# Transposing the MLP activations of a decoder trunk by transfers through a DRAM scratch

## The chip, the cores and the metric

One core of one Trainium2 chip runs the kernel. The metric is the device time of one execution in microseconds. Before the change three runs took 2196.67, 2196.99 and 2197.36 us; their median is 2196.99 us. A run-to-run difference of about 0.2% (4.4 us) is what a measurement of this kernel can tell from no change.

## What is computed

The reference is a decoder trunk of two layers over 256 tokens of width 2048, in float32. Each layer does a self-attention, a cross-attention over 256 memory tokens, and a squared-ReLU MLP with 8192 hidden columns; each is pre-normed and added to the residual stream. The change touches the MLP alone:

```python
def sq_relu_mlp(h, wup, wdown):
    return jnp.square(jax.nn.relu(h @ wup)) @ wdown
...
x = x + sq_relu_mlp(rms_norm(x, mlp_norm[i]), mlp_wup[i], mlp_wdown[i])
```

The product with `wup` leaves tokens on the partitions and hidden columns along the row. The product with `wdown` sums over hidden columns, so TensorE wants these on the partitions: each activated tile of 128 tokens x 512 hidden columns has to be turned between the two.

## The kernel before

**Arithmetic.** Every float32 matrix is held as two parts, a high one (`hi`, the value rounded to the type that TensorE reads in one pass) and a low one (`lo`, value minus `hi`), and a product is three matmuls: hi x hi, hi x lo, lo x hi. ScalarE (ACT) makes the high part of a weight by a cast (`whi`, line 219), VectorE (DVE) the low part by a subtraction (`wlo`, line 220). A weight tile `raw` of 128 x 2048 elements (1 MB) gives two such *pieces* of 128 x 1024 each. There are seven `raw` buffers, and four buffers for each of `whi` and `wlo`, so ACT and DVE run at most four pieces ahead of TensorE. Transfers of weights are issued by SyncE (SP) in program order (`load`, line 187); some 1 MB transfers that add onto a loaded tile are issued by GpSimd (POOL, lines 840 and 964).

**The MLP.** The hidden columns are worked in eight blocks `b` of 1024, each of two chunks `c` of 512, for two token tiles `t` of 128. Block 0 is done plainly. Blocks 1 to 7 use seven products in place of eight (class `Seven`, products `p1` to `p7` in the order p1 p1 p5 p5 p6 p3 p6 p3 p2 p7 p2 p7 p4 p4, two steps each; a step is two pieces of six matmuls). Sums of the products leave four activated tiles in each block, in the order p6, p1, p5, p4. The down product of earlier blocks (`mm` in a profile's rows, twelve matmuls for each piece) is laid between the steps of `Seven` (`pr`).

**The activated tile.** `out` (in `mlp`, lines 1403 to 1428) starts one task for each activated tile. The task does ReLU and a square on ACT (lines 1416 and 1417; the name of a tile tells its product, p6 for example, which the profile shows as `p`), waits some planned time, takes a free PSUM bank, turns the tile by four transposes of 128 x 128 on TensorE (`transpose4`, lines 372 to 376; `flip`, line 172), and reads the bank into the two parts of a tile `unit` (`split`, lines 360 to 365: a cast on ACT, line 364, and a subtraction on DVE, line 365). Down products that come later read this `unit`.

**What sets the order.** TensorE's order is written out by the program: side tasks such as `out` say with `yield` how long they mean to wait on a planned clock (`T_SQ`, `T_TURN` and so on), and are stepped in between matmuls when that time has come. The instructions of the other engines are put in order by a scheduler with its own idea of their durations; each engine then takes its queue strictly in order. SP's weight loads keep the program's order among themselves. Small float32 tiles (activated tiles among them) come from seven rotating buffers, tag `ev`.

Of the kernel before, what the change touches and what calls it, by code (L numbers as in the profile page):

```python
# [10 lines left out]
F32 = mybir.dt.float32  # L11
F32R = mybir.dt.float32r
I32 = mybir.dt.int32
AF = mybir.ActivationFunctionType
ALU = mybir.AluOpType
AX = mybir.AxisListType

P = 128
# [3 lines left out]
CH = 512  # L22
# [4 lines left out]
LAST = MLP_BLOCKS - 1  # L27
SEVEN = (1, 2, 3, 4, 5, 6, 7)
SPREAD = {("p1", 1), ("p5", 1), ("p6", 0), ("p6", 1), ("p2", 0), ("p2", 1), ("p7", 1)}
EVS = 7  # L30
WEAVE = "A1", "A2", "A5", "A3", "A6 B1", "A7 B2", "A4", "B5", "B3", "B6", "B7", "B4"
CLOSING = "u A1 u A2 B1 u A5 B2 u B5 u A6 u A3 B6 u B3 u A7 A4 u B7 u B4"

T_EV, T_TURN, T_ROT, T_SM, T_SQ, T_ADD, T_NORM, T_SUM = 2.6, 2.6, 12.0, 6.5, 4.4, 2.2, 7.2, 3.0

URGENT = 250
NEG = -1.0e30
# [14 lines left out]
def trunk(ctx, tc, x, xT, xT0, mem, memT, positions, gcols, gfinal, lam_vecs, consts, W, out):  # L52
    nc = tc.nc

    def pool(name, bufs, space=None):
        kw = {"space": space} if space else {}
        return ctx.enter_context(tc.tile_pool(name=name, bufs=bufs, **kw))
# [5 lines left out]
    work = pool("work", 2)  # L63
    small = pool("small", 3)
    banks = pool("banks", 8, bass.MemoryType.PSUM)

    serial = [0]

    def nm(s):
        serial[0] += 1  # L70
        return f"{s}_{serial[0]}"
# [102 lines left out]
    def f32(ap):  # L174
        return ap.bitcast(F32)
# [173 lines left out]
    g = keep.tile([P, NG], F32, name="g")  # L349
    pos = keep.tile([P, NT], I32, name="pos")  # L350
    lamv = work.tile([P, 4, P], F32, tag="ev", name="lamv", bufs=EVS)
# [8 lines left out]
    def split(dst, t, src):  # L360

        n = src.shape[1]
        hi = dst[:, 0, :n, t * P : (t + 1) * P]
        nc.scalar.copy(hi, src)  # L364
        nc.vector.tensor_tensor(dst[:, 1, :n, t * P : (t + 1) * P], src, f32(hi), ALU.subtract)  # L365

    def scaled(src, cols, tmp=None):
        if tmp is None:
            tmp = work.tile([P, 4, P], F32, tag="ev", name=nm("xg"), bufs=EVS)
        nc.vector.tensor_tensor(tmp, src, cols.unsqueeze(2).broadcast_to([P, 4, P]), ALU.mult)  # L370
        return tmp

    def transpose4(src, pt):

# [20 lines left out]
    def given_tile(dst, k, raw, gain):  # L395
        nc.scalar.activation(dst[:, 0, k], raw, AF.Copy, scale=gain)
        given_low(dst, k, raw, gain)
# [5 lines left out]
    def sum_squares(acc, src, scale=1.0):  # L403
        junk = work.tile([P, CH], mybir.dt.bfloat16, tag="junk", name=nm("junk"), bufs=1)
        return nc.scalar.activation(junk[:, : src.shape[1]], src, AF.Square, scale=scale, accum_out=acc)  # L405

# [121 lines left out]
    def evacuate(ps, scale):  # L528
        e = work.tile([P, CH], F32, tag="ev", name=nm("ev"), bufs=EVS)
        nc.scalar.activation(e[:, : ps.shape[1]], ps, AF.Copy, scale=scale)  # L530
        return e
# [868 lines left out]
    def mlp(l, norm, gnext):  # L1400
        a = norm.done()
        rstd = keep2(norm.rstd, 1.0, "r1")
        hid = {}

        chunk = {}
        sums = {}
        copied = {}

        def out(b, c, t, src, r, wait):

            if (b, c) not in hid:
                hid[b, c] = Held(unit())
            dst = hid[b, c]

            def task():
                nc.scalar.activation(r, src, AF.Relu, scale=rstd[t])
                nc.scalar.activation(r, r, AF.Square)
                yield wait
                pt = yield from side_bank()
                pt = transpose4(r, pt)  # L1420
                if b < LAST or (t, c) != (1, 0):
                    split(dst, t, pt)
                if b == LAST:
                    pair.keep(t, c, pt)
                yield T_TURN
                give_back()

            dst.run(task())

        def finish_chunk(of, ps, landed):  # L1430
            for t in range(NT):
                if of.kind == "up":
                    r = work.tile([P, CH], F32, tag="ev", name=nm("ev"), bufs=EVS)
                    out(*of.halves[0], t, ps[t], r, T_SQ)
                else:
                    add_residual(t, of.c, ps[t])
                    if landed:
                        landed(of.c, t, ps[t], True)

        def acts_of(of):  # L1440
            if of.kind == "up":
                return [a.unit_of(u) for u in range(4)]
            return [hid[k] for k in of.halves]

        def run(line, landed=None):
            for item in line:
                of = item.of
                if item.early:
                    item.early(hid)
                if isinstance(of, Seven):  # L1450
                    of.products(
                        a, item.u, copied,
                        lambda t, c, src, r, b=of.b: out(b, c, t, src, r, T_SQ + 7.0),
                    )
                    continue
                if isinstance(of, Pair):
                    of.products([hid[LAST, c] for c in range(2)], item.u, landed)
                    continue
                n = len(of.all)
                if item.u == 0:  # L1460
                    if of.open:
                        sums[of.kind, of.c] = [bank("mm") for _ in range(NT)]
                    chunk["acts"] = acts_of(of)
                act = chunk["acts"][item.u]
                need(act.tasks)
                for h, (hi, lo) in enumerate(take()):
                    for t in range(NT):
                        unit_part(sums[of.kind, of.c][t], act, h, hi, lo, t, of.open and item.u == 0, of.close and item.u == n - 1)
                if item.u == n - 1 and of.close:
                    finish_chunk(of, sums.pop((of.kind, of.c)), landed)  # L1470

        line, end, pair = mlp_lines[l]
        limit = free_banks[0] - 1
        free_banks[0] -= limit
        run(line)

        def last(nxt):
            left = {(c, t): 1 for c in range(4) for t in range(NT)}
            for item in end:
                if isinstance(item.of, Pair):  # L1480
                    for t, j, _ in Pair.ADDS[item.u]:
                        left[item.of.cols[j], t] += 1

            def landed(c, t, ps, alone, side=None):
                if side == 0:
                    assert left[c, t] == 1
                    nxt(c, t, ps, side)
                    return
                left[c, t] -= 1
                if not left[c, t]:  # L1490
                    assert alone
                    nxt(*((c, t, ps) if side is None else (c, t, ps, side)))

            run(end, landed)
            assert not any(left.values())
            free_banks[0] += limit

        if gnext is None:
            return last
        nxt = Stream(gnext)  # L1500
        last(nxt.feed)
        return nxt
# [344 lines left out]
```

## Time and profile before

| | |
|---|---|
| median of three runs | 2196.99 us |
| the profiled execution | 2197.04 us |
| its span, first to last instruction | 2195.3 us |
| granted TensorE clock, mean | 0.999 |
| TensorE matmuls busy | 2184.3 us (100%) |
| VectorE busy | 1742.1 us (79%) |
| ScalarE busy | 1409.1 us (64%) |
| GpSimd busy | 177.1 us (8%) |
| DMA, two main queues | 51.3% and 19.9% of 16 engines' time |

Times in the rows are from the start of the span. In a timeline a row gives start, length, engine, source line, operation, tiles (output <- inputs), how many were merged, and in brackets the idle time before it with what ended it. Matmuls overlap in the pipe, so the distance between two starts tells how long TensorE gives to one, and not the length of a row. `SPq` is SP's queue of issues. A table of windows gives the busy time of each engine in a stretch. In the list of transfers the last number is the median time from issue to landing.

### The profile page before, as it was taken

Reading aid. Unit: us, or ns where it says so; the run is one execution under the profiler, and the core shown is the slowest. Engines: PE = TensorE matmul, PEld = TensorE weight load, DVE = VectorE, ACT = ScalarE, POOL = GpSimd, SP = SyncE. Lnnn points to the kernel's source line nnn. Section 1 sums busy time; section 2 is a strip of 40 time slices with the busy share of each in tenths; the row PEclk is TensorE's granted clock in tenths of the full one; section 3 lists DMA queues with packets and bytes.
Section 4 is the critical chain, followed back from the end, with each engine's and each line's share of the span. In section 5 each row is a group of like instructions: output and inputs, shape, how many; then the busy total and the mean of one; then the engine's idle time right before and its main releaser. Section 6 shows DMA issues by size and latency. Waiting matters only on the chain.

```text
span 2195.3 us, 27641 instructions
## 1 busy us (share of the span) xinstructions
PE 2184.3 (100%) x10451; PEld 1831.1 (83%) x10451; DVE 1742.1 (79%) x1962; ACT 1409.1 (64%) x1872; POOL 177.1 (8%) x270
## 2 busy tenths in 40 slices
PE   9999999999999999999999999999999999999998
PEld 7888888888888888888889988888888888888887
DVE  6665878788888788878886878778887887888887
ACT  7555656666766766666765755556766667666665
POOL 1112210000000000000000320000000000000001
PEclk9999999999999999999999999999999999999999
DMA  9447796447967887797996344635878679779795
GB/s 384 157 158 251 213 292 235 159 153 242 310 210 228 294 236 227 266 278 229 294 252 221 105 165 155 248 127 184 266 262 265 203 284 288 212 242 294 230 311 149
DMA packets 76886, 509.28 MB, mean 232 GB/s; under 512 B 8784, under 2 KB 9168, under 8 KB 17872
## 3 DMA queue, kind: packets, MB, share of 16 engines
q1 hardware_dynamic: 64800, 422.83, 51.3%
q0 software_dynamic: 11520, 83.89, 19.9%
q8 instruction: 82, 1.34, 0.2%
q10 hardware_dynamic: 432, 0.79, 0.1%
q14 instruction: 52, 0.43, 0.1%
HBM read 505.38 MB, written 2.10 MB: 231 GB/s over the span
## 4 chain that ended last, share of the span: by engine, by line
PE 98%; DVE 1%; DMA 0%; issue 0%; ACT 0%; DVEq 0%; POOLq 0%; POOL 0%
PE mm L168 63%; PE pr L168 29%; PE ax L168 3%; PE ax L172 2%; PE mm L172 1%; DVE wlo L220 0%; DMA raw<-in_mlp_wup_dram 0%; DMA raw<-in_da_wqkv_dram 0%; DVE x L525 0%; PE pr L172 0%; ACT whi L219 0%; DVE p L651 0%; DVE raw L848 0%; DVE ev L1662 0%; ACT p L590 0%
## 5 line engine op out<-in xcount | busy, mean ns | idle before, releaser
L220 DVE TENSOR_TENSOR wlo<-raw,whi 128x1024 fp32r<-128x1024 f32 (+3 forms) x946 | 1139.1, 1215 | 370.2 <-ACT whi L219 344.5
L219 ACT CAST whi<-raw 128x1024 fp32r<-128x1024 f32 (+2 forms) x945 | 987.0, 1045 | 651.2 <-PE mm L168 501.9
L168 PE MATMUL mm<-whi,unit 128*128 128x512 f32 (+2 forms) x4000 | 1276.5, 389 | 0.3 <-DVE whi L216 0.3
L168 PEld LDWEIGHTS mm<-whi,unit 128*128 128x128 f32 x4000 | 748.6, 188 | 148.2 <-ACT unit L1217 1.2
L168 PE MATMUL mm<-wlo,unit 128*128 128x512 f32 (+2 forms) x2000 | 772.6, 387 | 0.0
L168 PE MATMUL pr<-whi,unit 128*128 128x512 f32 x1912 | 619.3, 391 | 0.0
L168 PEld LDWEIGHTS mm<-wlo,unit 128*128 128x128 f32 x2000 | 375.9, 188 | 70.5 <-DVE wlo L220 0.8
L168 PEld LDWEIGHTS pr<-whi,unit 128*128 128x128 f32 x1912 | 358.5, 188 | 73.3
L168 PE MATMUL pr<-wlo,unit 128*128 128x512 f32 x956 | 371.6, 389 | 0.2 <-DVE wlo L220 0.2
L168 PEld LDWEIGHTS pr<-wlo,unit 128*128 128x128 f32 x956 | 179.7, 188 | 36.9 <-DVE wlo L220 1.0
L840 POOL DMA_DIRECT2D raw<-in_mlp_wup_dram x48 | 42.6, 887 | 915.2 <-DVE wlo L220 731.4
L848 DVE TENSOR_TENSOR raw<-raw,raw 128x2048 f32<-128x2048 f32 x40 | 91.4, 2286 | 6.4 <-DMA raw<-in_mlp_wup_dram 6.0
L525 DVE TENSOR_TENSOR x<-x,mm 128x512 f32<-128x512 f32 x128 | 84.5, 679 | 7.8 <-PE mm L168 7.7
L411 POOL TENSOR_TENSOR rs<-rs,mhalf 128x1 f32<-128x1 f32 (+1 forms) x26 | 24.4, 945 | 598.8 <-DVE rs L410 598.8
L220 DVE TENSOR_TENSOR wlo<-unit,whi 128x1024 fp32r<-128x1024 f32 x48 | 57.9, 1220 | 1.9
L219 ACT CAST whi<-unit 128x1024 fp32r<-128x1024 f32 x48 | 50.7, 1056 | 12.5 <-PE pr L168 12.2
L168 PE MATMUL mm<-unit,whi 128*128 128x256 f32 x256 | 46.9, 284 | 0.0
L172 PEld LDWEIGHTS ax<-identr,p 128*128 128x128 f32 x304 | 37.9, 139 | 10.1
L172 PE MATMUL ax<-identr,p 128*128 128x128 f32 x304 | 46.1, 271 | 0.0
L365 DVE TENSOR_TENSOR unit<-ax,unit 128x512 fp32r<-128x512 f32 x66 | 45.0, 685 | 1.3 <-ACT unit L364 1.0
L364 ACT CAST unit<-ax 128x512 fp32r<-128x512 f32 x66 | 38.1, 581 | 11.7 <-PE ax L172 11.7
L405 ACT ACTIVATE junk<-x 128x512 bf16<-128x512 f32 (+1 forms) x57 | 35.3, 620 | 9.6 <-DVE x L1053 5.2
(191 smaller groups left out, 1232.5 us busy)
## 6 DMA issues: line engine op xcount, KB each, us to landing
raw<-in_mlp_wdown_dram SPq DMA_DIRECT2D x128, 1024.0 KB, 7.1
raw<-in_mlp_wup_dram SPq DMA_DIRECT2D x120, 1024.0 KB, 6.9
raw<-in_mlp_wup_dram POOLq DMA_DIRECT2D x48, 1024.0 KB, 8.8
raw<-in_da_wqkv_dram SPq DMA_DIRECT2D x45, 1024.0 KB, 7.5
raw<-in_da_wo_dram SPq DMA_DIRECT2D x16, 1024.0 KB, 6.8
raw<-in_ca_wkv_dram SPq DMA_DIRECT2D x16, 1024.0 KB, 4.9
raw<-in_mlp_wdown_dram POOLq DMA_DIRECT2D x16, 1024.0 KB, 10.6
raw<-in_mla_wo_dram SPq DMA_DIRECT2D x16, 1024.0 KB, 5.5
```

The lines of the kernel that those rows point to most:

```text
L168: return nc.tensor.matmul(o, stationary, moving, start=start, stop=stop, skip_group_check=onto)
L172: nc.tensor.transpose(o, src, ident)
L219: nc.scalar.copy(hi, r)
L220: nc.vector.tensor_tensor(lo, r, f32(hi), ALU.subtract)
L364: nc.scalar.copy(hi, src)
L365: nc.vector.tensor_tensor(dst[:, 1, :n, t * P : (t + 1) * P], src, f32(hi), ALU.subtract)
L405: return nc.scalar.activation(junk[:, : src.shape[1]], src, AF.Square, scale=scale, accum_out=acc)
L411: nc.gpsimd.tensor_tensor(r[:, :n], r[:, :n], mhalf.broadcast_to([P, n]), ALU.pow)
L525: nc.vector.tensor_tensor(xc, xc, ps, ALU.add)
L840: tc.keep_in_program_order(nc.gpsimd.dma_start(onto, src, accum_op=ALU.add))
L848: nc.vector.tensor_tensor(o, o, q, ALU.add)
```

## The change

For 26 of the 32 activated tiles of each layer (all of blocks 1 to 6, and chunk 0 of block 0) the turn by TensorE is replaced:

1. `half_words`: ACT copies the squared tile, seen as 128 x 1024 words of 16 bits, into two planes (low halves, high halves) of 512 words each; POOL issues a transfer of the 256 KB to a DRAM scratch tile `turned` of 256 x 512 words.
2. The task waits a planned 12.5 us (`T_STORE`).
3. `turned_by_dma`: SP issues a transposing transfer of the scratch tile into `landed` (128 x 4 x 256 words; pairs of words are again float32 values), and `split` reads `landed` in place of the PSUM bank.
4. The task waits a planned 6.5 us (`T_DMA`).

`planes` and `landed` come from the same seven `ev` buffers; the scratch has six buffers. The other 6 tiles of each layer keep TensorE's turn.

```diff
+U16 = mybir.dt.uint16
...
-T_EV, T_TURN, T_ROT, T_SM, T_SQ, T_ADD, T_NORM, T_SUM = 2.6, 2.6, 12.0, 6.5, 4.4, 2.2, 7.2, 3.0
+T_EV, T_TURN, T_ROT, T_SM, T_SQ, T_ADD, T_NORM, T_SUM, T_STORE, T_DMA = 2.6, 2.6, 12.0, 6.5, 4.4, 2.2, 7.2, 3.0, 12.5, 6.5
...
     banks = pool("banks", 8, bass.MemoryType.PSUM)
+    turned = pool("turned", 6, bass.MemoryType.DRAM)
...
+    def half_words(src):
+        planes = work.tile([P, 2, CH], U16, tag="ev", name=nm("planes"), padded_shape=[P, 2, CH], bufs=EVS)
+        nc.scalar.copy(planes, src.bitcast(U16).rearrange("p (w s) -> p s w", s=2))
+        there = turned.tile([2 * P, CH], U16, tag="turned", name=nm("turned"))
+        nc.gpsimd.dma_start(there.rearrange("(q s) w -> q s w", s=2), planes)
+        return there
+
+    def turned_by_dma(there, dst, t):
+        landed = work.tile([P, 4, 2 * P], U16, tag="ev", name=nm("landed"), bufs=EVS)
+        nc.sync.dma_start_transpose(landed, there)
+        split(dst, t, landed.bitcast(F32))
...
                 nc.scalar.activation(r, src, AF.Relu, scale=rstd[t])
                 nc.scalar.activation(r, r, AF.Square)
+                if b < LAST and (b, c) != (0, 1):
+                    there = half_words(r)
+                    yield T_STORE
+                    turned_by_dma(there, dst, t)
+                    yield T_DMA
+                    return
                 yield wait
```

The queues change at the same places in every block. The first place is ACT's queue around the tile p6 of block 3 in the first layer (in the profile of before this stands at 718 to 732 us). Before, with `whi` the pieces of weights:

```order
L219 CAST whi_1220_6207<-raw_1167_5950 128x1024
L1416 ACTIVATE p6_1216_6201<-p6_1216_6201,r1_890_4476 128x512
L219 CAST whi_1222_6211<-raw_1167_5950 128x1024
L1417 ACTIVATE p6_1216_6201<-p6_1216_6201 128x512
L219 CAST whi_1224_6240<-raw_1219_6205 128x1024
L219 CAST whi_1226_6244<-raw_1219_6205 128x1024
L219 CAST whi_1231_6267<-raw_1230_6265 128x1024
L219 CAST whi_1233_6271<-raw_1230_6265 128x1024
L219 CAST whi_1235_6287<-raw_1185_6041 128x1024
L364 CAST unit_1228_6261<-ax_1248_6355 128x4x128
```

And the same place of the changed kernel (its piece whi_1244 is whi_1224 of before, and so on; `landed` is the tile that the transposing transfer writes):

```order
L221 CAST whi_1240_6219<-raw_1187_5965 128x1024
L1430 ACTIVATE p6_1236_6213<-p6_1236_6213,r1_890_4478 128x512
L221 CAST whi_1242_6223<-raw_1187_5965 128x1024
L1431 ACTIVATE p6_1236_6213<-p6_1236_6213 128x512
L377 COPY planes_1249_6276<-p6_1236_6213 128x1024
L221 CAST whi_1244_6252<-raw_1239_6217 128x1024
L221 CAST whi_1246_6256<-raw_1239_6217 128x1024
L221 CAST whi_1253_6283<-raw_1252_6281 128x1024
L366 CAST unit_1248_6273<-landed_1270_6377 128x4x128
L221 CAST whi_1255_6287<-raw_1252_6281 128x1024
```

The copy of the planes is new behind the square, and the read of the turned tile stands two pieces earlier, with three pieces between it and the copy.

The second place is SP's queue of issues at the same time. Before (`unit_1250` and the `raw` tiles behind it are weights of the next block and of the down product):

```order
L187 DMA raw_1239_6319<-in_mlp_wdown0_dram 128x2048
L187 DMA unit_1250_6372<-in_mlp_wup0_dram 128x2048
L187 DMA raw_1255_6406<-in_mlp_wup0_dram 128x2048
L187 DMA raw_1256_6408<-in_mlp_wup0_dram 128x2048
L187 DMA raw_1261_6434<-in_mlp_wup0_dram 128x2048
L187 DMA raw_1267_6478<-in_mlp_wdown0_dram 128x2048
```

And in the changed kernel:

```order
L189 DMA raw_1261_6335<-in_mlp_wdown0_dram 128x2048
L384 DMA_TRANSPOSE landed_1270_6377<-turned_1250_6278 128x4x256
L189 DMA unit_1274_6389<-in_mlp_wup0_dram 128x2048
L189 DMA raw_1279_6423<-in_mlp_wup0_dram 128x2048
L189 DMA raw_1280_6425<-in_mlp_wup0_dram 128x2048
L189 DMA raw_1287_6455<-in_mlp_wup0_dram 128x2048
L384 DMA_TRANSPOSE landed_1292_6490<-turned_1273_6387 128x4x256
L189 DMA raw_1293_6496<-in_mlp_wdown0_dram 128x2048
```

The transposing transfer of p6 stands ahead of the next block's four loads, and that of p1 ahead of the load of a `wdown` tile (raw_1293, which is raw_1267 of before). Each waits for its store.

The third place is POOL's queue, where the stores stand among the adding transfers. Before:

```order
L840 DMA raw_1167_5950<-in_mlp_wup0_dram 128x2048
L840 DMA raw_1185_6041<-in_mlp_wup0_dram 128x2048
L840 DMA unit_1250_6372<-in_mlp_wup0_dram 128x2048
L840 DMA raw_1255_6406<-in_mlp_wup0_dram 128x2048
L840 DMA raw_1283_6551<-in_mlp_wup0_dram 128x2048
```

And in the changed kernel (`turned` is the scratch tile that a store writes):

```order
L854 DMA raw_1205_6053<-in_mlp_wup0_dram 128x2048
L379 DMA turned_1250_6278<-planes_1249_6276 128x1024
L379 DMA turned_1273_6387<-planes_1272_6385 128x1024
L854 DMA unit_1274_6389<-in_mlp_wup0_dram 128x2048
L379 DMA turned_1286_6453<-planes_1285_6451 128x1024
L854 DMA raw_1279_6423<-in_mlp_wup0_dram 128x2048
```

The stores of p6 and p1 now stand ahead of the adding transfer onto the next block's first tile, and the store of p5 ahead of the second one.

## The prediction

> **What bounds the kernel now.** I read the page's shares first, then its chain, then one block of the MLP at close range: a table of windows and the engines' timelines.
>
> ```profile
> PE 2184.3 (100%) x10451; PEld 1831.1 (83%) x10451; DVE 1742.1 (79%) x1962; ACT 1409.1 (64%) x1872; POOL 177.1 (8%) x270
> PE 98%; DVE 1%; DMA 0%; issue 0%; ACT 0%; DVEq 0%; POOLq 0%; POOL 0%
> ACT whi L219 <- PE mm L168: 501.9, 405, 2.7
> 720.00:800.00 80.00, 80.00 (x362) 66.19 (x362) 67.09 (x59) 53.57 (x59) 3.53 (x4) 1.00 0.80 259
> ```
>
> TensorE is the bound: 98% of the chain, and busy for 80.00 of 80 us in this stretch of one block, where DVE (67.09), ACT (53.57) and the DMA engines (0.80) have room. The third row says who paces whom: ACT waits for TensorE to free a weight buffer, 501.9 us in all. So each TensorE instruction taken out shortens the time by itself, until a piece of weights comes late.
>
> **What is removed.** The turn of one tile, in TensorE's timeline (start, length):
>
> ```profile
> 719.38 0.39 PE L168 MATMUL mm<-whi,unit 128*128 128x512 f32 x1
> ...
> 724.82 0.39 PE L168 MATMUL pr<-whi,unit 128*128 128x512 f32 x1
> ...
> 728.91 0.60 PE L172 MATMUL ax<-identr,p 128*128 128x128 f32 x4
> 729.26 0.48 PE L168 MATMUL pr<-whi,unit 128*128 128x512 f32 x1
> ...
> 730.74 0.40 PE L168 MATMUL mm<-whi,unit 128*128 128x512 f32 x1
> ```
>
> From 719.38 to 724.82 stand 24 matmuls: 5.44 us, 0.227 each. From 724.82 to 730.74 stand 24 matmuls and the four transposes: 5.92 us. A turn costs 0.48 us of TensorE. The condition in the change holds for 2 + 6 x 4 = 26 tiles a layer, 52 in all: 52 x 0.48 = **25.0 us** off. Nothing else on TensorE moves.
>
> **What is added, and the first place: ACT's queue.** ACT's timeline around p6 of block 3:
>
> ```profile
> 719.18 0.72 ACT L1416 ACTIVATE p<-p,r 128x512 f32<-128x512 f32 x1
> 719.80 1.04 ACT L219 CAST whi<-raw 128x1024 fp32r<-128x1024 f32 x1
> 720.75 0.62 ACT L1417 ACTIVATE p<-p 128x512 f32<-128x512 f32 x1
> 722.30 1.05 ACT L219 CAST whi<-raw 128x1024 fp32r<-128x1024 f32 x1 [0.93 <-PE mm L168]
> 725.02 1.05 ACT L219 CAST whi<-raw 128x1024 fp32r<-128x1024 f32 x1 [1.67 <-PE mm L168]
> 726.38 1.06 ACT L219 CAST whi<-raw 128x1024 fp32r<-128x1024 f32 x1 [0.30 <-PE pr L168]
> 727.74 1.06 ACT L219 CAST whi<-raw 128x1024 fp32r<-128x1024 f32 x1 [0.30 <-PE pr L168]
> ```
>
> The copy of the planes has no row. Below it cannot be under the 0.62 us of a 512-element square; a copy of 1024 elements to another type, the cast, takes 1.05, and twice that (2.1) bounds it from above if 16-bit words at a stride go at half speed. I take 1.05, the same count of elements. It runs 721.37 to 722.42. Fifty-two of them are 55 us on an engine that idles 26 of 80 us here: covered, at nothing. The read of the turned tile costs ACT and DVE what the read of PSUM did (a cast and a subtraction of 512 columns): nothing.
>
> The new wait is dangerous by what is queued behind it. In the new order ACT casts three pieces (rows 722.30, 725.02, 726.38) and then stands at the turned tile; the piece of row 727.74 comes behind. TensorE starts the preceding piece at 730.74 and, with twelve matmuls, needs that fourth one at 730.74 + 12 x 0.227 = 733.46, its low part 0.23 later. Behind the turned tile's landing ACT needs 0.6 for its cast and 1.06 for the piece, then DVE 1.23 for the low part:
>
> ```profile
> 734.81 1.23 DVE L220 TENSOR_TENSOR wlo<-raw,whi 128x1024 fp32r<-128x1024 f32 x1 [1.06 <-ACT whi L219]
> ```
>
> So the tile may land until 733.69 - 2.9 = 730.8 without a wait on TensorE: **8.4 us** behind the end of the planes. By the order, ten tiles (p6 of blocks 1 to 4 and the second tile of block 0, both layers) have three pieces between; four (p6 of blocks 5 and 6) have one twelve-matmul piece more and 11.1 us; p1 has five or six (10.8 to 12.1 us); p5 and p4 have eight or nine (16 us and more). The data themselves are first multiplied over 20 us of matmuls later, so only the queues can hurt.
>
> **Store and transposing transfer.** Neither has a row. The nearest ones are transfers of 256 KB, with the median from issue to landing, and POOL's issues:
>
> ```profile
> out_dram<-x SPq DMA_DIRECT2D x7, 256.0 KB, 2.7
> raw<-in_memT_dram SPq DMA_DIRECT2D x16, 256.0 KB, 3.1
> x<-in_x_dram SPq DMA_DIRECT2D x8, 256.0 KB, 10.7
> raw<-in_mlp_wup_dram SPq DMA_DIRECT2D x120, 1024.0 KB, 6.9
> 712.95 0.89 POOL L840 DMA_DIRECT2D raw<-in_mlp_wup_dram  x1 [11.14 <-DVE wlo L220]
> 730.58 0.88 POOL L840 DMA_DIRECT2D unit<-in_mlp_wup_dram  x1 [16.74 <-DMA unit<-in_mlp_wup_dram]
> ```
>
> The store goes from SBUF to DRAM like the output's 2.7 us; on POOL I add its 0.9 us of issue: 3.6, up to 10.7 + 0.9 in a crowded queue. POOL is free at 722 (rows 712.95 and 730.58), so the store lands at 722.5 + 3.6 = 726.1. The transposing transfer I put at memT's 3.1, a 256 KB load from DRAM issued by SP; its ends are 2.7 and 10.7. It lands at 729.2, or **6.8 us** behind the planes: 1.6 us to spare at the tight ten. The quiet rows are nearer than the crowded 10.7, which is the prologue's: SP's next transfers stand behind this one, so at 722 to 729 nothing new is in its way:
>
> ```profile
> 725.02 0.33 SPq L187 DMA_DIRECT2D unit<-in_mlp_wup_dram  x1
> 725.45 2.24 SPq L187 DMA_DIRECT2D raw<-in_mlp_wup_dram  x3
> 730.08 0.33 SPq L187 DMA_DIRECT2D raw<-in_mlp_wdown_dram  x1
> ```
>
> One rule can be set beside this. The Trainium skill's DMA: Bandwidth & Descriptors, section Latency and other measured facts, gives transposing transfers 261 GB/s, by which 256 KB would take an estimated 1.0 us of moving; no run here shows it, and it would leave the sum as it is.
>
> **The second place: SP's queue.** SP issues in order, and a transposing transfer waits for its store. That of p6 holds the next block's loads (rows 725.02 and 725.45) until 726.1, one microsecond. That of p1 stands ahead of the down weight that was issued at 730.08. The rows that matter, of ACT, of TensorE, and the span of landings of the six loads that SP issued from 729 to 753 us:
>
> ```profile
> 734.68 0.62 ACT L1417 ACTIVATE p<-p 128x512 f32<-128x512 f32 x1
> 752.01 1.03 ACT L219 CAST whi<-raw 128x1024 fp32r<-128x1024 f32 x1
> 756.20 0.39 PE L168 MATMUL mm<-whi,unit 128*128 128x512 f32 x1
> DMA to landing us min/median/max: 10.9/14.4/19.6
> ```
>
> The square of p1 ends at 735.30, its planes at 736.4; its store lands 0.1 + 3.6 later, at 740.1, and the load can go at 740.4, ten microseconds later than before. It is read at 752.01, and TensorE first needs the piece at 756.20, the low part 0.23 later: the read may slip to 756.43 - 1.23 - 1.06 = 754.1. That leaves the load 13.7 us. Before, it took the 19.6 us, since two adding transfers and four other loads filled the engines; in the new order these adding transfers come later (next paragraph), and 6.9 us is the median of such loads. I cost it at nothing; above 13.7 us each microsecond counts in all 12 blocks.
>
> **The third place: POOL's queue.** Two adding transfers now stand behind stores.
>
> ```profile
> 741.46 0.63 ACT L1417 ACTIVATE p<-p 128x512 f32<-128x512 f32 x1
> 733.05 0.87 POOL L840 DMA_DIRECT2D raw<-in_mlp_wup_dram  x1 [1.60 <-DVE p L920]
> 755.04 1.06 ACT L219 CAST whi<-unit 128x1024 fp32r<-128x1024 f32 x1
> 759.12 1.06 ACT L219 CAST whi<-raw 128x1024 fp32r<-128x1024 f32 x1 [1.19 <-PE mm L168]
> raw<-in_mlp_wup_dram POOLq DMA_DIRECT2D x48, 1024.0 KB, 8.8
> unit<-in_mlp_wup_dram POOLq DMA_DIRECT2D x8, 1024.0 KB, 12.2
> ```
>
> The first, of 730.58, waits for the store of p1 to be issued, until 737.3; with 12.2 us it lands at 749.5 and is read at 755.04. The second, of 733.05, waits for the store of p5 (its square ends at 742.1, its planes at 743.1, and POOL's issue of the store at 744.1); with 8.8 it lands at 753 and is read at 759.12. Both are hidden with over five microseconds to spare. With them the pipe is free for the loads at 725 to 737, which is what pays for the later load above.
>
> **The sum.** It is made against the profiled execution: 2197.04 us, a span of 2195.3 and 1.7 around it, which the change leaves alone; that is the median of the runs (2196.99) within 0.1. Off: 25.0. On: at the ten tight places 1.6 us are to spare; a copy at its upper end takes 1.05 of it, and store and transfer spread by 0.4 each (2.7 to 3.1), so I allow 0.2 us at each, 2 us. 2197.0 - 25.0 + 2 = **2174 us**.
>
> **Rivals.**
>
> *The turned tile lands late and ACT's queue blocks.* This is the one that ends slower. Place: the piece behind the landed tile; point: 8.4 us behind the planes. A landing at L costs 10 x (L - 8.4), and from 10.8 and 11.1 on also at p1's (six with 10.8, six with 12.1, and two first tiles of block 0 with 10.8) and the four with 11.1. At L = 10.9 that is the 25 us gained, so it is slower from there. With a transposing transfer of 8 us, L = 11.7: 33 + 2 + 7 = 42 on, **2214 us**; with the crowded row's 10.7, L = 14.4: 60 + 13 + 29 + 14 = 116 on, 2288 us. For it: no row shows such a transfer. Against it: all quiet rows of 256 KB lie at 3 us. A rule of the Trainium skill speaks for it: VectorE: DVE Perf Modes, section The three transpose paths, has 1309 ns for a 128x128 square of two-byte words by the transfer's crossbar against 390 ns on TensorE, and advises TensorE where PSUM will do. Eight such squares make one tile here, an estimated 10.5 us if they add up, near the crowded row. On TensorE the trace differs from the page: 0.48 us for four turns. For the transfers no row decides; the skill's other figure, the 261 GB/s above, would have the squares overlap. 22%.
>
> *SP's loads come late.* Place: the load behind p1's transposing transfer; point: 13.7 us. At the 14.4 of the row above 0.7 x 12 = 8 us on, 2180; at the 19.6, 5.9 x 12 = 71 on, **2243**. Against it: the adding transfers leave the stretch. 12%, mostly small.
>
> *The transposing transfer fills the DMA engines.* The engines are busy for 0.80 x 80 = 64 us of a block:
>
> ```profile
> q1 hardware_dynamic: 64800, 422.83, 51.3%
> ```
>
> At this queue's rate (422.83 MB in 51.3% of 2195 us, 0.375 MB/us) 256 KB take 0.7 us; four stores are 2.8, and 13.2 are left for four transposing transfers, 3.3 each. Cut into small pieces they could take more; at 6.9 us, as long as a load of four times the size takes to land, 3.6 x 4 x 13 blocks = 187 on, **2359**. 8%.
>
> That the tiles are still turned on TensorE as before is excluded by the order, which has 52 rows of transposes less. That DVE takes over as the bound is excluded by its 67.09 of 80 us, which the change doesn't raise.
>
> **Chances and range.** The forecast 58%: 2168 to 2184. The first rival 22%: 4 still faster, 6 within 0.2%, 12 slower. The second 12%: 4, 2 and 6. The third 8%, slower. That makes 66% for faster by over 0.2% (4.4 us, about what a measurement can tell from no change), 8% for within, 26% for slower. The range goes from 2166 (the 25 us whole, with a few from adding transfers that no longer crowd loads) to 2214, the first rival at 8 us; above stays what is left of the slow cases, some 16%.
>
> **What would show it.** TensorE's group of transposes of `p` and `ev` has 208 fewer rows; the chain stays 98% TensorE. Right: the store lands 3.6 us and the transposing transfer about 3 us behind its issue, and ACT's waits for `landed` are a microsecond or less. Wrong by the first rival: ACT or DVE waits of some microseconds at the cast of `landed`, and TensorE idle behind `whi` or `wlo` once in each block. By the second: ACT waits for a `wdown` transfer in each block. By the third: the DMA share near full for whole blocks.

## The result, and the profile after

| | before | after |
|---|---|---|
| median of four runs each, us | 2196.83 | 2211.55 |
| lowest and highest | 2196.64, 2197.36 | 2208.88, 2214.58 |
| the profiled execution, and its span | 2197.04, 2195.3 | 2211.45, 2209.7 |
| TensorE matmuls | 10451 | 10243 |
| adding transfers of POOL for `wup`, median to landing | 8.8 | 9.4 |

The change makes the kernel slower: the ratio is 1.0067, with a 95% interval from 1.005 to 1.0084. Faster was forecast. A few executions of the kernels below came out over 1.5% above the fastest of their kernel, and the medians leave them out. From the page, the engines, the two main DMA queues, and the chain of work that ended last:

```profile
PE 2174.6 (98%) x10243; PEld 1813.1 (82%) x10243; DVE 1737.5 (79%) x1962; ACT 1446.9 (65%) x1924; POOL 207.5 (9%) x322
q1 hardware_dynamic: 119712, 436.47, 54.8%
q0 software_dynamic: 15680, 97.53, 21.7%
PE 60%; issue 25%; DMA 10%; DVE 2%; POOL 1%; ACT 1%; SPq 0%; POOLq 0%; DVEq 0%; ACTq 0%
```

The 208 transposes are gone. TensorE's busy time fell by only 9.7 us of the 25 (a matmul row's length, and so the busy time, holds some waiting in the pipe), and the chain, 98% TensorE before, is 60% now. A table of windows of the MLP, with the same columns as before (the last three are the granted clock, the DMA engines' share, and GB/s), and the waits that are new, with total, count and longest:

```profile
640.00:720.00 80.00, 78.46 (x346) 64.31 (x345) 66.84 (x59) 56.76 (x64) 5.85 (x8) 1.00 0.93 281
800.00:880.00 80.00, 78.44 (x338) 64.19 (x337) 64.68 (x57) 55.35 (x62) 5.89 (x9) 0.98 0.90 270
1970.00:2050.00 80.00, 72.04 (x304) 58.24 (x303) 57.63 (x51) 51.58 (x58) 5.78 (x8) 0.94 0.94 254
```
```profile
ACT unit L366 <- DMA landed<-turned: 57.5, 26, 10.2
ACT whi L221 <- DMA raw<-in_mlp_wdown_dram: 19.7, 12, 3.7
PE pr L170 <- ACT whi L221: 12.3, 6, 7.5
PE pr L170 <- DVE wlo L222: 9.9, 14, 1.6
```

TensorE, which hardly paused here before (79.78 us busy of 80 in the last window, 80.00 in the other two), now waits for weight pieces, and ACT waits for `landed`, the turned tile. (Source lines stand 2 to 14 later than before; line 366 is the cast in `split`.) The place is not where the prediction looked. ACT and SP around the tiles p6 and p1 of block 4:

```profile
811.81 0.63 ACT L1431 ACTIVATE p<-p 128x512 f32<-128x512 f32 x1
812.47 1.05 ACT L377 COPY planes<-p 128x1024 uint16<-128x1024 uint16 x1
...
821.08 1.05 ACT L221 CAST whi<-raw 128x1024 fp32r<-128x1024 f32 x1 [0.30 <-PE mm L170]
825.66 0.62 ACT L366 CAST unit<-landed 128x512 fp32r<-128x512 f32 x1 [3.53 <-DMA landed<-turned]
826.18 3.88 ACT L221 CAST whi<-raw 128x1024 fp32r<-128x1024 f32 x4
```
```profile
802.34 1.23 SPq L384 DMA_TRANSPOSE landed<-turned  x1
803.68 5.15 SPq L189 DMA_DIRECT2D raw<-in_mlp_wup_dram  x4
818.17 2.64 SPq L384 DMA_TRANSPOSE landed<-turned  x1
820.90 0.53 SPq L189 DMA_DIRECT2D raw<-in_mlp_wdown_dram  x1
```

The transposing transfer of 802.34 is that of p6; it lands 3.3 us later, as forecast. The one of 818.17 is that of p1: its planes end at 813.52, and ACT stands until it lands at 825.6, 12.1 us behind the planes and 7.5 behind its issue. The four pieces behind it come late, and TensorE pauses, and then runs some ten matmuls at half its pace (the last row is a window, with a granted clock of 0.57):

```profile
826.09 0.39 PE L170 MATMUL pr<-whi,unit 128*128 128x512 f32 x1
827.27 0.50 PE L170 MATMUL pr<-whi,unit 128*128 128x512 f32 x1 [0.80 <-ACT whi L221]
828.53 0.50 PE L170 MATMUL pr<-wlo,unit 128*128 128x512 f32 x1 [0.76 <-DVE wlo L222]
828.87 0.86 PE L170 MATMUL pr<-whi,unit 128*128 128x512 f32 x2
829.54 0.63 PE L170 MATMUL pr<-wlo,unit 128*128 128x512 f32 x1
...
829.00:833.00 4.00, 4.00 (x13) 3.08 (x12) 4.00 (x4) 3.26 (x6) 0.00 (x0) 0.57 0.94 197
```

Two neighbouring matmuls start 0.227 us apart, and after this stall 0.43. I summed what neighbours are apart beyond 0.227, where it is over 0.12, in the MLP's 490 to 1040 and 1560 to 2080 us: 35.5 us, against 0.4 before. Followed back through the waits, 22.3 of it ends at a late `landed` (all but 1.4 at p1), 5.2 at late `wup` loads, 1.4 at late `wdown` loads, and 6.7 are matmuls at the slow pace. 35.5 - 0.4 - 25.0 = 10.1 of the 14.4 us by which the span grew. Gaps of 0.10 to 0.12 us, which this sum leaves out and most of which stand right behind these stalls, hold 2.9 us more (0.2 before); the last 1.6 are not located.

What sets the 7.5 us shows when the 52 transposing transfers are set beside the adding transfers of POOL: 28 had none in flight beside them and landed in 3.2 to 4.9 us; 24 had one or two and took 5.4 to 13.0. In block 4:

```profile
813.88 0.57 POOL L379 DMA_DIRECT2D turned<-planes  x1 [13.43 <-ACT planes L377]
814.65 0.90 POOL L854 DMA_DIRECT2D raw<-in_mlp_wup_dram  x1 [0.20 <-issue]
821.13 0.56 POOL L379 DMA_DIRECT2D turned<-planes  x1 [5.58 <-ACT planes L377]
821.85 0.89 POOL L854 DMA_DIRECT2D raw<-in_mlp_wup_dram  x1 [0.17 <-issue]
```

Behind p1's store POOL issues an adding transfer (line 854; it lands at 824.6), and behind p5's store a second (833.5). They fall on p1's transposing transfer in every block, and the second on nearly all of p5's.

### The profile page after: what moved, and what is told of

Read it like the earlier page. It is cut to its first block, busy times and chain, and to the rows that moved or that the text cites. A ratio compares the mean times of both kernels' runs of the same rounds, so it can differ in the third digit from the quotient of the medians.

```text
span 2209.7 us, 27532 instructions
## 1 busy us (share of the span) xinstructions
PE 2174.6 (98%) x10243; PEld 1813.1 (82%) x10243; DVE 1737.5 (79%) x1962; ACT 1446.9 (65%) x1924; POOL 207.5 (9%) x322
## 4 chain that ended last, share of the span: by engine, by line
PE 60%; issue 25%; DMA 10%; DVE 2%; POOL 1%; ACT 1%; SPq 0%; POOLq 0%; DVEq 0%; ACTq 0%
PE mm L170 44%; PE pr L170 11%; DMA raw<-in_mlp_wup_dram 4%; DMA landed<-turned 3%; DMA turned<-planes 3%; PE ax L170 2%; DVE wlo L222 1%; PE ax L174 1%; DMA raw<-in_mlp_wdown_dram 1%; PE mm L174 1%; POOL raw L854 1%; ACT whi L221 1%; SPq L384 0%; POOL turned L379 0%; DMA raw<-in_xT_dram 0%
## 5 line engine op out<-in xcount | busy, mean ns | idle before, releaser
L170 PE MATMUL pr<-wlo,unit 128*128 128x512 f32 x956 | 376.1, 393 | 10.0 <-DVE wlo L222 9.9
L379 POOL DMA_DIRECT2D turned<-planes x52 | 29.5, 567 | 548.7 <-ACT planes L377 548.7
L366 ACT CAST unit<-landed 128x512 fp32r<-128x512 f32 x52 | 32.3, 620 | 60.1 <-DMA landed<-turned 57.5
L367 DVE TENSOR_TENSOR unit<-landed,unit 128x512 fp32r<-128x512 f32 x52 | 35.8, 689 | 40.6 <-ACT unit L366 40.4
L377 ACT COPY planes<-p 128x1024 uint16<-128x1024 uint16 x48 | 50.1, 1043 | 0.6
L1430 ACT ACTIVATE p<-p,r 128x512 f32<-128x512 f32 x42 | 30.4, 724 | 24.0 <-DVE p L934 11.6
## 6 DMA issues: line engine op xcount, KB each, us to landing
raw<-in_mlp_wdown_dram POOLq DMA_DIRECT2D x16, 1024.0 KB, 10.4
```

The costliest lines, as they stand in the source:

```text
L170: return nc.tensor.matmul(o, stationary, moving, start=start, stop=stop, skip_group_check=onto)
L377: nc.scalar.copy(planes, src.bitcast(U16).rearrange("p (w s) -> p s w", s=2))
L379: nc.gpsimd.dma_start(there.rearrange("(q s) w -> q s w", s=2), planes)
```

## The experiments

Each median stands beside runs of the kernel before on the same chip (2196.7 to 2197.1 in all groups); the ratio is to those.

**1 to 4: who reads, who turns.** The first theory, from the waits above, was that ACT's place is the cause (A); its rivals were SP's order (B) and full DMA engines (C).

p1 on TensorE again:
```diff
-                if b < LAST and (b, c) != (0, 1):
+                if b < LAST and (b, c) != (0, 1) and (b == 0 or (t, c) != (0, 0)):
```


> The 12 tiles p1 of blocks 1 to 6 are turned by TensorE again, the other 40 stay with the transfers. Theory A (ACT stands at the cast of p1's turned tile, which lands 11 to 20 us behind its planes): 40 x 0.48 = 19 us off, and of the 36 us of stalls in the changed kernel's trace the ones behind `landed` and the slow matmuls after them go, 7 us or less are left: 2178 to 2185 us. Theory B (SP's loads come late, since a transposing transfer holds SP's queue until its store has landed): three of four such waits stay in each block, and stalls behind `wup` and `wdown` loads remain or grow: 2190 to 2200. Theory C (the DMA engines are too full): three quarters of the stalls stay, 2196.8 - 19 + 27 = 2205.

Measured 2182.34, ratio 0.993 (0.9918 to 0.9942). This version beats both kernels. Its DMA engines are nearly as full as the changed kernel's (0.89 to 0.93 against 0.89 to 0.95 in the 80 us windows), so fullness alone is not the cause, and C falls in that form. The trouble hangs on p1.

p1 read later (`casts` lists ACT's casts of pieces, `n` is their number when p1's planes are made):
```diff
-        split(dst, t, landed.bitcast(F32))
+        with behind(cast):
+            split(dst, t, landed.bitcast(F32))
...
+                    n = len(casts)
                     yield T_STORE
-                    turned_by_dma(there, dst, t)
+                    turned_by_dma(there, dst, t, b and (t, c) == (0, 0) and casts[n + 5])
```


> All 52 tiles go by transfers as in the changed kernel; only the cast of p1's turned tile stands nine pieces of weights behind its planes on ACT in place of five or six. Theory A: p1's tile still lands 11 to 14 us behind its planes, ACT no longer waits there, and the 25 us come through but for some stalls behind loads: 2173 to 2181 us. Theory B: SP's queue is as before, the time stays at 2205 to 2212. Theory C: the same, 2205 to 2212.

Measured 2214.92, ratio 1.0081 (1.0056 to 1.0107). A falls. ACT's waits for `landed` shrink, and those for the load behind p1's transposing transfer in SP's queue take their place:

```profile
ACT unit L368 <- DMA landed<-turned: 25.3, 17, 5.4
ACT whi L223 <- DMA raw<-in_mlp_wdown_dram: 35.6, 11, 6.3
PE mm L170 <- ACT whi L223: 20.7, 7, 9.7
```

By the same sum of gaps, 29.7 us now end at `wdown` loads. ACT's wait had been a place where one delay showed, not its source.

Nothing reads the tiles:
```diff
-                    turned_by_dma(there, dst, t)
-                    yield T_DMA
-                    return
-                yield wait
+                    turned_by_dma(there, None, t)
+                else:
+                    yield wait
```


> All 52 tiles are copied, stored and transposed by transfers as in the changed kernel, but nothing reads the turned tiles: TensorE turns every tile, as before the change. Theory A: no cast waits for `landed`; what is left is the price of the transfers in the queues, the 7 us of stalls behind loads or less: 2197 to 2204 us. Theories B and C (the stalls come from SP's order or from full DMA engines, whoever reads the tiles): 2196.8 + 36 = 2225 to 2235.

Measured 2223.26, ratio 1.0117 (1.0087 to 1.0147). Once more against A: the transfers alone cost 26 us.

No turn at all (the 52 tiles are read as they lie, so the turn is left out of the computation):
```diff
-                    there = half_words(r)
-                    yield T_STORE
-                    turned_by_dma(there, dst, t)
-                    yield T_DMA
+                    yield T_STORE + T_DMA
+                    split(dst, t, r.rearrange("p (k t) -> p k t", t=P))
```


> The 52 tiles aren't turned at all: the cast and the subtraction read the squared tile where it lies, with no planes, no store and no transposing transfer, so that the part of the computation that is left out is the turn of these tiles. It gives the most that the change could bring. All theories: 52 x 0.48 = 25.0 us off, 2172 us; a result under 2168 would say that the transposes cost more than 0.48 us a tile, one over 2176 that they cost less.

Measured 2171.87, ratio 0.9884: 25.2 us off, against 25.0 by the sum. So the changed kernel, at 2211.55, loses 39.7 us elsewhere.

**5 to 8: the wait or the movement.** B was split in two: B1, SP's wait for p1's store; B2, the movement itself.

p1's transposing transfer behind the load (on top of the late read):
```diff
-                    yield T_STORE
+                    yield T_STORE + (3.0 if b and (t, c) == (0, 0) else 0.0)
```


> All 52 tiles by transfers, p1's read nine pieces behind its planes, and p1's transposing transfer now stands behind the load of the `wdown` tile in SP's queue in place of ahead of it (next in the queue is p5's transposing transfer, which waits longer still). Theory B1 (SP stands at the wait for p1's store, and the `wdown` load behind it is issued too late): the load goes out when it did before the change, nearly all of the 25 us come through: 2174 to 2182 us. Theory B2 (the 256 KB of p1's transposing transfer itself slow the loads, wherever it stands) or C (DMA engines too full): 2200 to 2220, as in the run that read the tiles late.

Measured 2289.77, ratio 1.0431 (1.0406 to 1.0457): far worse than either theory allowed, and the most telling trace of all. Block 4, first SP's and POOL's queues, then windows:

```profile
825.77 0.33 SPq L189 DMA_DIRECT2D raw<-in_mlp_wdown_dram  x1
835.19 20.87 SPq L386 DMA_TRANSPOSE landed<-turned  x2
856.15 0.53 SPq L189 DMA_DIRECT2D raw<-in_mlp_wup_dram  x1
```
```profile
829.05 0.90 POOL L857 DMA_DIRECT2D raw<-in_mlp_wup_dram  x1 [0.20 <-issue]
835.52 0.56 POOL L381 DMA_DIRECT2D turned<-planes  x1 [5.57 <-ACT planes L379]
836.24 0.89 POOL L857 DMA_DIRECT2D raw<-in_mlp_wup_dram  x1 [0.17 <-issue]
```
```profile
829.00:835.00 6.00, 6.00 (x28) 4.95 (x27) 4.74 (x5) 4.95 (x6) 0.90 (x1) 1.00 1.02 347
835.00:841.00 6.00, 6.00 (x28) 4.98 (x27) 4.56 (x5) 4.52 (x6) 1.44 (x2) 1.00 1.24 191
841.00:846.00 5.00, 5.00 (x24) 4.03 (x22) 2.05 (x2) 0.92 (x1) 0.00 (x0) 1.00 1.11 47
846.00:851.00 5.00, 0.27 (x2) 0.00 (x0) 0.00 (x0) 0.00 (x0) 0.00 (x0) 0.98 1.07 50
851.00:855.00 4.00, 0.00 (x0) 0.00 (x0) 0.00 (x0) 0.00 (x0) 0.00 (x0) 0.50 0.52 75
855.00:860.00 5.00, 1.02 (x2) 0.52 (x3) 1.96 (x3) 3.68 (x6) 0.00 (x0) 0.50 1.05 175
860.00:870.00 10.00, 10.00 (x35) 8.08 (x36) 9.33 (x9) 6.93 (x8) 0.56 (x1) 0.78 0.89 348
```

No load of SP is in flight after 836. What is: p1's transposing transfer of 835.19, 256 KB, which lands after 21.1 us; the store of 835.52, after 19.1; the adding transfer of 836.24, after 23.2. The engines are booked as busy (1.1) and move 47 GB/s where 347 had gone just before. From this came theory D: a transposing and an adding transfer in flight together hold each other up.

SP waits, and moves nothing (TensorE turns p1):
```diff
+                    tiny = work.tile([P, 4, 2 * P], U16, tag="ev", name=nm("tiny"), bufs=EVS)
+                    nc.sync.dma_start(tiny[0:1, 0, 0:64], there[0:1, 0:64])
```


> As the kernel with p1 turned by TensorE and the other 40 by transfers; besides, p1's planes are made and stored, and SP issues, in the place of p1's transposing transfer, a transfer of 128 bytes that reads the stored tile, so that SP waits for the store but moves next to nothing; nothing uses it. Theory B1: the wait alone makes the `wdown` load late: 2200 to 2215 us. Theory B2 or C: 2182 to 2186, as without p1's transfers.

Measured 2191.18, ratio 0.9977 (0.9968 to 0.9986): 8.8 us above the first experiment. SP's wait costs, but between the two bounds and far from the whole.

SP moves, and waits for nothing:
```diff
+                    landed = work.tile([P, 4, 2 * P], U16, tag="ev", name=nm("landed"), bufs=EVS)
+                    nc.sync.dma_start_transpose(landed, stored["p6"])
```


> As the run before it, but in the place of p1's transposing transfer SP issues a transposing transfer of p6's tile, stored 15 us earlier: the same 256 KB are moved and nothing is waited for; nothing uses them. Theory B1: 2182 to 2188 us. Theory B2 or C: 2200 to 2215.

Measured 2215.73, ratio 1.0084 (1.0067 to 1.0101): 33 us above the first experiment. (The issue of this transfer held SP too, for 7.6 us in block 3, but the `wdown` load behind it went out at 735.4, earlier than the 739.2 of experiment 6.) B1 falls as the main cause, and the movement it is.

p1 alone by transfers:
```diff
-                if b < LAST and (b, c) != (0, 1):
+                if 0 < b < LAST and (t, c) == (0, 0):
```


> Only the 12 tiles p1 go by transfers, the other 40 are turned by TensorE as before the change; its transposing transfer stands ahead of the `wdown` load as in the changed kernel. Theory B1: 12 x 0.48 = 6 us off and the wait of SP in each block as before, about 2 us of stalls in each: 2205 to 2215 us. If it takes full DMA engines as well (0.82 to 0.84 of their time here in place of 0.92), the load still goes out late but lands sooner: 2191 to 2196.

Measured 2242.04, ratio 1.0206 (1.0192 to 1.0219). Twelve tiles do more harm than 52, and the DMA engines are no fuller than before the change (0.77 to 0.83 of their time in the 80 us windows, against 0.79 to 0.81), so C falls altogether. D can explain it: with p5's store gone, POOL issues both adding transfers right behind p1's store, and the transposing transfer has both beside it for its whole time, in all twelve blocks.

**9 to 12: D by itself.** POOL's transfers write over the tile in place of adding:
```diff
-                tc.keep_in_program_order(nc.gpsimd.dma_start(onto, src, accum_op=ALU.add))
+                tc.keep_in_program_order(nc.gpsimd.dma_start(onto, src))
```


> The changed kernel, in which POOL's 1 MB transfers write over the loaded tile in place of adding onto it: the additions of weight tiles by these transfers are left out, and nothing else (the same queue, places, sizes and waits). Theory D (a transposing transfer and an adding transfer that are in flight together hold each other up): p1's transposing transfer lands within 3 to 5 us, the stalls go, 2172 to 2183 us. Theory E (it is the order of the queues, or what is in flight whatever it does): as the changed kernel, 2205 to 2215.

Measured 2179.85, ratio 0.9921 (0.9908 to 0.9933).

The same edit in the kernel of experiment 8, with p1 alone by transfers:

> The kernel with only p1 by transfers, in which POOL's 1 MB transfers write over the loaded tile in place of adding onto it (the additions by these transfers are left out). Theory D: the transposing transfers land in 3 to 7 us in place of 12 to 14, and the time falls from 2242 to 2191 to 2196 us, before the change less 12 x 0.48. Theory E: 2235 to 2245.

Measured 2191.7, ratio 0.9976 (0.9966 to 0.9986), 50 us less than with the additions. The landing of the transposing transfers (shortest, median, longest) in these two, the changed kernel, and the one with p1 alone:

```profile
DMA to landing us min/median/max: 3.1/3.4/6.5
```
```profile
DMA to landing us min/median/max: 6.0/7.9/8.7
```
```profile
DMA to landing us min/median/max: 3.2/4.7/13.0
```
```profile
DMA to landing us min/median/max: 11.9/12.8/14.0
```

Same queues, sizes and order; only the adding is gone, and with it 31.7 us of the changed kernel's 39.7. SP stands at p1's store as long as ever (12.6 us in block 3, 12.5 in the changed kernel). D holds. One part of its expectation was off: with p1 alone they still take 6.0 to 8.7, not 3 to 7, so a crowd costs something without any adding. In 14 us of block 3, from 1.5 us ahead of p1's transposing transfer, the engines are as busy in both (0.98 and 0.99), but move 206 GB/s with the adding and 365 without (first with it):

```profile
744.00:758.00 14.00, 14.00 (x66) 11.62 (x65) 11.90 (x12) 10.25 (x11) 1.50 (x2) 1.00 0.98 206
```
```profile
736.80:750.80 14.00, 14.00 (x66) 11.61 (x65) 11.90 (x12) 10.31 (x12) 0.81 (x2) 1.00 0.99 365
```

That the adding alone does not do this is seen in the kernel before, in the 14 us in which both adding transfers start beside plain loads, with no transposing one:

```profile
730.00:744.00 14.00, 14.00 (x65) 11.56 (x65) 9.82 (x12) 9.82 (x13) 1.75 (x2) 1.00 1.03 321
```

Can all 52 be kept, if the two kinds are kept apart in time? The tiles are first multiplied over 28 us after they are read, so there is room:
```diff
-                    yield T_STORE
+                    yield T_STORE + ({(0, 0): 24.0, (1, 1): 14.0}.get((t, c), 0.0) if b else 0.0)
...
+                    with behind(b and casts[-1]):
+                        split(dst, t, landed)
```


> All 52 tiles by transfers, with the adding transfers as they are; the transposing transfers of p1 and p5 are issued 24 and 14 us later, beside that of p4, where no adding transfer is planned, and all of blocks 1 to 6 are read behind the newest piece of weights. Theory D: nearly all transposing transfers land in 3 to 5 us and most of the 25 us come through: 2173 to 2184 us. Theory E: three of them on end in front of SP's loads cost more than they did: 2200 or more.

> As the run before it, with p1 30 us and p5 22 us later: p5 then stands with two more loads ahead of p1 and behind p4's place or beside it. Theory D: 2173 to 2184 us, as long as none is still in flight when the next block's adding transfers start (some 80 us after this block's first); if one is, a few us more. Theory E: 2200 or more.

Measured 2214.47 (1.0079, 1.0067 to 1.0091) and 2209.77 (1.006, 1.0048 to 1.0072): not what D alone promised. In both, no transposing transfer meets an adding one of the MLP, and they land in 3.0 to 8.3 us in the first (at most 10.5 in the second); but the stalls are there, 21 us of them behind `wup` loads. SP's queue in block 3 of the first, with one store of POOL:

```profile
749.73 0.33 SPq L189 DMA_DIRECT2D raw<-in_mlp_wdown_dram  x1
758.23 0.56 POOL L381 DMA_DIRECT2D turned<-planes  x1 [9.45 <-ACT planes L379]
764.70 1.71 SPq L386 DMA_TRANSPOSE landed<-turned  x1
766.52 0.52 SPq L189 DMA_DIRECT2D raw<-in_mlp_wup_dram  x1
```

SP issues nothing for 15 us. The transposing transfer of 764.70 is p4's: with p1's and p5's put off, it is the first of the three in SP's queue, and it waits for its own store, that of 758.23, which lands at 764.69. The loads behind it, which the kernel before issued from 750 on, go out from 766 on. In all twelve blocks SP issues nothing for 11 to 17 us ahead of it, against 7 to 12 in the changed kernel. Some of the cost had moved from the DMA engines to SP's queue.

**13 and 14: less of both.** The three late transposing transfers now stand behind three or four more loads, with 36, 28 and 12 us in the diff above for p1, p5 and p4 (experiment 13), or 40, 33 and 20 (experiment 14):

> All 52 tiles by transfers and all adding transfers as they are. The transposing transfers of p1, p5 and p4 are issued 36, 28 and 12 us later than planned in the changed kernel: in SP's queue 11 or 12 loads now lie between p6's and them, in place of 8, so that p4's store has landed when SP comes to them. Theory D with SP's wait as the second cost: no transposing transfer beside an adding one, no load held: 2173 to 2182 us. If the waits of SP are not what is left (theory E: their mere presence among the loads costs it): 2200 or more, as in the two runs before.

> The same with 40, 33 and 20 us: one load more ahead of the last two in half of the blocks. Theory D with SP's wait: 2173 to 2182 us, or some microseconds more where a transposing transfer runs into the next block's first adding transfer. Theory E: 2200 or more.

Measured 2193.79 (0.9987, 0.9978 to 0.9996) and 2203.35 (1.0029, 1.0018 to 1.0041). The first gains 20.7 us on experiment 11, but lies 12 us above the range expected. SP's queue is not free in it, though that was expected. In block 3 the `wup` load that went out at 766.5 goes out at 753.2 now, but SP then stands 6.6 us until p4's store has landed (6 to 8 us in eight of the twelve blocks), and takes 10.7 us to issue the three transposing transfers:

```profile
760.08 10.65 SPq L386 DMA_TRANSPOSE landed<-turned  x3
```

That the gain comes from SP's shorter stand is argued, not shown, since the transfers moved as well. Its stalls, 18.4 us, end mostly behind `wup` loads of the crowded middle of a block, which land 16 to 26 us behind their issue in block 3.

**15: the stores alone.** TensorE turns all, no transposing transfer is issued:
```diff
-                    turned_by_dma(there, dst, t)
-                    yield T_DMA
-                    return
-                yield wait
+                else:
+                    yield wait
```


> ACT makes the planes of the 52 tiles and POOL stores them, but no transposing transfer is issued and TensorE turns every tile as before the change. If the stores alone make the crowded stretch too full: 2203 us or more. If it takes the transposing transfers (which came to 2223 with these stores): 2197 to 2200.

Measured 2197.8, ratio 1.0008 (0.9999 to 1.0017): planes and stores are free by themselves, and all but 1 of the 26 us of the run without readers belong to the transposing transfers.

## Why the prediction was wrong, step by step

- *What is removed, 25.0 us.* Right: 25.2 without any turn.
- *What is added on ACT.* Right: 52 copies of 1.05 us, covered.
- *The first place, p6.* Right: store and transposing transfer take the forecast time (802.3 to 805.6 in block 4), planes to landing 5.9 to 7.7 us where 6.8 was forecast and 8.4 the limit; all pauses of TensorE behind `landed` in blocks 1 to 6 belong to p1.
- *"The transposing transfer I put at memT's 3.1".* **This is the step that failed.** 3.1 is right for p6 and was carried to p1, where the transfer takes 6.6 to 8.2 us and once 13.0. p1's store, put at 3.6 from its issue, is late too, by less: 4.0 to 6.3 us in ten of twelve. So the tile lands 10.4 to 13.7 us (once 19.6) behind the planes, against limits of 10.8 and 12.1. The prediction held both halves of the cause and never laid them side by side: in its second place p1's transposing transfer starts at 740.1 (measured in the changed kernel: 740.6), and in its third place the adding transfer goes out at 737.3 (736.8) and lands at 749.5 (747.1). The times were right to two or three microseconds, and they overlap. It asked of the adding transfer only whether *it* comes in time.
- *The third place, costed at nothing.* Right for the adding transfer's own reader, wrong for its neighbour: by experiment 9 this meeting is worth 31.7 us.
- *The second place, SP's queue, costed at nothing.* Too low. The load went out at 742.3, not 740.4, 0.5 us for the later store, and the rest since the issue of a transposing transfer holds SP, for 1.2 to 2.6 us in the changed kernel. SP's wait at p1 is worth 8.8 us (with p1's planes and store) in experiment 6, and as soon as ACT is freed (experiment 2) the load behind it is what comes late.
- *The rivals.* The first had the mechanism of the visible stall (ACT's cast of `landed`) and, at 8 us of transfer, 2214, close to the 2211.6 measured. That closeness is luck: 33 of its 42 us were put at the ten tight tiles, where nothing stalled but 1.4 us in block 0, and curing ACT cured nothing. The third, full engines, had the right quarter and the wrong reason: the share rose from 0.80 to some 0.92, but experiment 1 loses little at that share, and experiment 8 loses most at the old one. By the Trainium skill's figure in VectorE: DVE Perf Modes, section The three transpose paths, of 1309 ns a square, which the prediction weighed, eight squares one behind the other would take an estimated 10.5 us; a tile with no adding transfer beside it lands in 3.2 to 4.9, so the squares overlap.
- *What stays open:* 1.6 us of the span; why the two kinds of transfer hold each other up inside the engines (the runs show that they do, and that the adding is needed; q1 has 54,912 more packets than before, 1056 for each transposing transfer, but no run shows whether that matters); and the last 22 us between experiment 13 and the time without any turn, of which only the place, late loads behind SP's stand and in the crowded stretch, is seen.

## What to carry to other kernels

Price an added transfer by what is in flight at its own time and place, not by the quiet row of its kind: lay its start and end beside those of every other transfer that the same change moves. When a wait is found ahead of a stall, take the wait away and see whether the time follows; here it went to the next queue, and only removing one property of the neighbour (the adding) moved it. And change the few bad cases, not the whole: 40 of the 52 turns by transfer gain 14.7 us, the other twelve lose 29.

## What the runs showed of the hardware

- A transposing transfer of 256 KB lands in 3.2 to 4.9 us with no adding transfer in flight beside it, in 5.4 to 13.0 beside one or two of 1 MB, in 12 to 14 where it has two beside it from start to end (experiment 8), and in up to 27.9 in experiment 5, where the moved bytes fall from 347 to 47 GB/s while the engines are booked as busy. With plain writes in place of the adding the worst of 52 is 6.5.
- The issue of a transposing transfer holds SP for 1.23 us at the least, and up to 7.7 (experiment 7); that of a 1 MB load takes 0.33 at the least, and up to 5.5 (experiment 8).
- The Trainium skill's DMA: Bandwidth & Descriptors, section Rules for kernel authors, says that a transpose next to ordinary DMAs needs nothing. Of correctness no run here says otherwise; of time, the rows above do for adding ones.
- TensorE's granted clock fell to 0.50 after some 5 us without work (window 851 to 855 above) and was back only in the course of 860 to 870; three of the changed kernel's stalls, one of them of only 2 us, at 827, were also followed by eight to eleven matmuls 0.43 us apart (granted clock 0.57 in 829 to 833), while those at 908 and 1721, of 2.5 to 2.7 us, were not. So a stall can cost more than its length: 6.7 of the changed kernel's 35.5 us are such matmuls.
